# Matrix memory on one Trainium2 core: the key weights multiplied into the query weights on the chip

## The chip, the cores and the metric

One core of a Trainium2 chip (trn2) runs the whole program in one launch. The metric is the device time of one launch in microseconds; each measurement is the median of several runs. Five engines work side by side: TensorE (PE; its weight loads are listed as PEld), VectorE (DVE), ScalarE (ACT), GpSimd (POOL) and SyncE (SP), whose queue issues most DMAs.

## The reference

A trunk of two layers over 1024 tokens with 1024 features, in float32. The first layer has two mixers behind one input projection: a matrix memory (mLSTM, four heads of 256) and a pooling over trailing windows of 2, 4, 8 and 16 tokens (four groups of 256). The second layer is latent attention; the change does not touch it. What matters of the first layer:

```python
xc = silu(causal_conv(xm, conv_w, conv_b))          # per head h: (S, 256)
q = xc_h @ w_q[h]
k = xc_h @ w_k[h] * 256 ** -0.5
v = xm_h @ w_v[h]
# per chunk of tokens, with decays from the gates:
s = (q @ k.T) * exp(dmat - m_t)
num = s @ v + w_inter * (q @ C);   den = rowsum(s) + w_inter * (q @ n)
C_new = wc * C + (k * ws).T @ v;   n_new = wc * n + sum(k * ws)
h = num / max(|den|, exp(-m_t))
h = rms_norm(h * sigmoid(om)) ;    ya = (h + skip * xc) * silu(zm)
```

## The kernel before

*Numbers in two parts.* Every operand of a large matmul is held as a high part `hi` (float32r) and the remainder `lo`. `mm3` (L172) issues three matmuls for a product: hi*hi, hi*lo and lo*hi. Data in SBUF are split by `split` (POOL writes `hi`, DVE the remainder), data in PSUM by `split_psum` and `split_scaled` (ACT writes `hi`, DVE the remainder).

*Weights.* `wload` (L182) takes a staging tile, sends a DMA on SP's queue and splits the block on POOL and DVE. In this layer there are two staging tiles and three tiles each for `hi` and `lo`, used in turn. `head_w` (L681) loads the 256 x 256 matrix of a head.

*Projections.* `feat_pieces` (L320) gives 128 columns of the input projection, in two pieces of 24 matmuls (512 tokens each). It is a generator: each `run(gen, n)` issues n pieces more, so that pieces can stand between other steps. `fill` holds the four pieces of the pooled input (`xp_pieces`), `zp_pieces` two per feature tile of the pooling gate, `xm_pieces` the memory's input, `zm_pieces` its gate; `om_tile` makes the output gate, 24 matmuls of 256 columns for each of eight token tiles.

*Heads and chunks.* The loop at L684 runs over the heads 3, 2, 1, 0. A head has two chunks of 512 tokens. `conv` makes `xc` (features on partitions), `Chunk.v` the values, `Chunk.kq` keys and queries (24 + 24 matmuls of 512 columns over both chunks, `k_ps` and `q_ps`), `decay` the exponentials, `scores` the lower triangle of the scores (`s_ps`), `update` the state after the first chunk: it transposes the keys (`kT_ps`), weights them and multiplies them with the values (`st`). `outputs` multiplies scores with values (`n_ps`), in the second chunk also queries with the state (`i_ps`), and normalises; `turn` transposes the result (`hT_ps`) and adds the skip. `windows` computes the trailing means on POOL and DVE, `pool_out` multiplies them with the group's weights (`pool_ps`).

*PSUM.* Two pools: `pmm` with five tiles for products and `ptr` with three for transposes.

*Order.* The program's text gives priorities. A planner with a simulated timeline (`schedule_with_timeline_sim`) sets the order on each engine from them, so instructions that are ready in its simulation can pass others; on the chip each engine then runs its list in order. Buffers are given out in the order of the text, and a tile's next user waits for its last reader.

The calls of a head whose order is changed, before:

```python
        c0.v(x_0, wv)
        ch_0 = c0.split_x(xc0)
        x_1 = c0.split_x(xm[:, :, 3 + HALF:3 + S])
        wq, wk = head_w("a_w_q", h), head_w("a_w_k", h)
        c0.kq(ch_0, wk, wq)
        skip_scale(h, xc0)
        c0.decay(); run(fill, 1); c0.scores()
        upd = c0.update(); run(upd, 1); run(fill, 1); run(upd)
        c0.outputs(sig); run(fill, 1)
        ...                                  # chunk 1: wv, wq, wk loaded again
        run(zp_pieces(g, 0, zs)); c1.scores()
        pool_out(g, 0, wg, mixes, zs); c1.outputs(sig)
```

The functions with the profile's line numbers:

Of the kernel before, what the change touches and what calls it, by code (L numbers as in the profile page):

```python
# [56 lines left out]
def _parts(value, bits, n):  # L57
    """value as a sum of n numbers of at most `bits` significant bits each."""
    from fractions import Fraction
    out = []  # L60
    rest = value
    top = 0
    while Fraction(2) ** (top + 1) <= rest:
        top += 1
    lsb = top - bits + 1
    for _ in range(n):
        unit = Fraction(2) ** lsb
        q = int(rest / unit)
        out.append(float(q * unit))
        rest -= q * unit  # L70
        lsb -= bits
    return out
# [16 lines left out]
def _hybrid(ctx, tc, nc, ins, consts, out, dbg):  # L89
# [20 lines left out]
    # ---------------------------------------------------------------- constants  # L110
# [5 lines left out]
    rows = cp.tile([P, P], F32, name="rows")  # L116
# [22 lines left out]
    def load_columns():  # L139
# [23 lines left out]
    def split_scaled(hi, lo, src, scale):  # L163
        """src * scale = hi + lo; src in PSUM, scale a number or a column."""
# [7 lines left out]
    def mm3(acc, terms, start=True, stop=True):  # L172
        """acc (+)= sum of lhs.T @ rhs over terms ((lhs_hi, lhs_lo), (rhs_hi, rhs_lo))."""
# [8 lines left out]
    def wload(shape, src, hi_eng="pool", own=None, into=None):  # L182
        """A block of weights, or of other operands, loaded and split."""
# [25 lines left out]
    def rstd_of(dst, ssq, n):  # L209
        """dst = (ssq / n + eps) ** -0.5 for small tiles."""  # L210
# [7 lines left out]
    # ================================================================ layer A  # L218
# [29 lines left out]
    def om_tile(h, sig, ws, j):  # L248
        """sigmoid(om) of a head for 128 tokens; with the last head's columns the gates too."""
# [12 lines left out]
    # ---- x normalised, transposed and split, and the first head's output gate on its heels  # L262
    with pool("xload") as tp:
# [43 lines left out]
        for j in range(NT):  # L307
# [5 lines left out]
            if j == 5:  # L313
                load_columns()
# [5 lines left out]
    def feat_pieces(c0, use, w=None):  # L320
        """128 columns of the projection, features on partitions: use(half, psum) per half."""
# [16 lines left out]
    def xm_pieces(h, xm, ws=(None, None)):  # L338
        V.memset(xm[:, :, 0:3], 0.0)
        for f in range(2):  # L340
            def use(half, ps):
                A.copy(xm[:, f, 3 + half * HALF:3 + (half + 1) * HALF], ps[:])
            yield from feat_pieces(A_XM + h * HD + f * P, use, ws[f])

    def new_xm():
        xm = hp.tile([P, 2, 3 + S], F32, name="xm", tag="xm", bufs=1)
        return xm

    def conv(h, c, xm):
        """SiLU of the causal convolution of a chunk."""  # L350
        t0 = c * HALF
        xc = hp.tile([P, 2, HALF], F32, name="xc", tag="xc", bufs=2)
        for f in range(2):
            ft = 2 * h + f
            acc = xc[:, f, :]
            A.activation(acc, xm[:, f, t0 + 3:t0 + 3 + HALF], AF.Identity,
                         bias=gcol("conv_b", ft), scale=gcol("conv_w", 3 * 8 + ft))
            for tap in range(3):
                V.scalar_tensor_tensor(acc, xm[:, f, t0 + tap:t0 + tap + HALF], gcol("conv_w", tap * 8 + ft),
# [4 lines left out]
    def xp_pieces(g, x0s):  # L364
        for f in range(2):
            x0 = hp.tile([P, PAD + S], F32, name="px", tag="px", bufs=2)
# [7 lines left out]
    def windows(g, x0s, half):  # L374
        """Trailing means less the value itself, split, for half of the tokens."""
# [44 lines left out]
    def gate_math():  # L420
# [4 lines left out]
        # Scratch in the room of tiles that come later.  # L425
# [13 lines left out]
        # log_sigmoid(f) = min(f, 0) - log1p(exp(-|f|))  # L439
# [10 lines left out]
        # Sums of log f within a tile of 128 tokens, and over whole tiles.  # L450
# [19 lines left out]
        # The running maximum within a tile, one (tile, head) per partition; then over tiles.  # L470
# [26 lines left out]
        # Exponents of the decay that depend on the query, as rows.  # L497
# [16 lines left out]
        # Weights of the first chunk's tokens in the state, and of the state later.  # L514
# [11 lines left out]
    # The next weights land behind x; their split stays behind x's work too.  # L526
# [8 lines left out]
    class Chunk:  # L535
        """One head's mLSTM over 512 tokens, step by step."""
# [6 lines left out]
        def split_x(self, src):  # L543
            xh = hb.tile([P, 2, HALF], F32R, name="xh", tag="xh", bufs=2)
            xl = hb.tile([P, 2, HALF], F32R, name="xl", tag="xl", bufs=2)
            for f in range(2):
                split(xh[:, f, :], xl[:, f, :], src[:, f, :])
            return xh, xl

        def v(self, xhl, wv):  # L550
            """Values, tokens on partitions, with a column of ones for the denominators."""
# [4 lines left out]
            V.tensor_copy(vl[:, :, HD:HD + 2], vzero[:].unsqueeze(1).broadcast_to([P, 4, 2]))  # L556
            for jj in range(2):
# [7 lines left out]
            self.vh, self.vl = vh, vl  # L565

        def kq(self, chl, wk, wq):
            ch, cl = chl
            self.qh = qh = hb.tile([P, 2, HALF], F32R, name="qh", tag="qh", bufs=1)
            self.ql = ql = hb.tile([P, 2, HALF], F32R, name="ql", tag="ql", bufs=1)  # L570
            self.kh = kh = hb.tile([P, 2, HALF], F32R, name="kh", tag="kh", bufs=1)
            self.kl = kl = hb.tile([P, 2, HALF], F32R, name="kl", tag="kl", bufs=1)
            if self.c == 0:
                self.kf = kf = hb.tile([P, 2, HALF], F32, name="kf", tag="hs", bufs=1)
            for f in range(2):
                fs = slice(f * P, (f + 1) * P)
                ps = pmm.tile([P, 512], F32, name="k_ps", tag="mm")
                mm3(ps[:], [((wk[0][:, k, fs], wk[1][:, k, fs]), (ch[:, k, :], cl[:, k, :])) for k in range(2)])
                if self.c == 0:
                    A.activation(kf[:, f, :], ps[:], AF.Copy, scale=HD ** -0.5)  # L580
                    split(kh[:, f, :], kl[:, f, :], kf[:, f, :])
                else:
                    split_scaled(kh[:, f, :], kl[:, f, :], ps[:], HD ** -0.5)
                ps = pmm.tile([P, 512], F32, name="q_ps", tag="mm")
                mm3(ps[:], [((wq[0][:, k, fs], wq[1][:, k, fs]), (ch[:, k, :], cl[:, k, :])) for k in range(2)])
                split_psum(qh[:, f, :], ql[:, f, :], ps[:])

        def decay(self):
            """exp of the decays' exponents, zero above the diagonal; keys on partitions."""
# [20 lines left out]
        def update(self):  # L610
            """The state after the first chunk."""
            h, kf, vh, vl = self.h, self.kf, self.vh, self.vl
            sth = hb.tile([P, 2, HD + 2], F32R, name="sth", tag="sth", bufs=1)
            stl = hb.tile([P, 2, HD + 2], F32R, name="stl", tag="stl", bufs=1)
            kwh = hb.tile([P, 4, HD], F32R, name="kwh", tag="kh", bufs=1)
            kwl = hb.tile([P, 4, HD], F32R, name="kwl", tag="kl", bufs=1)
            for i in range(4):
                pt = ptr.tile([P, 512], F32, name="kT_ps", tag="tr")
                for f in range(2):
                    T.transpose(pt[:, f * P:(f + 1) * P], kf[:, f, i * P:(i + 1) * P], ident[:])  # L620
# [12 lines left out]
        def outputs(self, sig):  # L633
            """Gated head outputs, tokens on partitions, and their norms."""
# [3 lines left out]
            for j in range(4):  # L638
# [8 lines left out]
                if self.state is not None:  # L647
                    sth, stl = self.state
                    pi = pmm.tile([P, 512], F32, name="i_ps", tag="mm")
# [12 lines left out]
                A.activation(sq[:], hs[:, j, :], AF.Square, accum_out=ssq[:, j:j + 1])  # L662
            rs = hb.tile([P, 4], F32, name="h_rs", tag="h_rs", bufs=2)
# [4 lines left out]
        def turn(self, xc):  # L668
            """Normalised outputs to features on partitions, plus the skip."""
# [13 lines left out]

    for h in reversed(range(M_HEADS)):  # L684
# [7 lines left out]
        x_0 = c0.split_x(xm[:, :, 3:3 + HALF])  # L692
        xc1 = conv(h, 1, xm)
        if h == M_HEADS - 1:
# [8 lines left out]
        c0.v(x_0, wv)  # L703
        ch_0 = c0.split_x(xc0)
        x_1 = c0.split_x(xm[:, :, 3 + HALF:3 + S])
        wq, wk = head_w("a_w_q", h), head_w("a_w_k", h)
        c0.kq(ch_0, wk, wq)
        skip_scale(h, xc0)
        c0.decay()
        run(fill, 1)  # L710
        c0.scores()
        upd = c0.update()
        run(upd, 1)
        run(fill, 1)
# [12 lines left out]
        skip_scale(h, xc1)  # L727
# [15 lines left out]
    # ---- output projection of layer A, half of the tokens at a time  # L743
# [35 lines left out]
    def norm_stats(tp, srcs):  # L779
        """Four tiles of 128 tokens, normalised in place."""  # L780
# [9 lines left out]
    def norm_turn(srcs, gname, hi_of, lo_of):  # L790
        """... and transposed, with a gain per feature, to hi_of(k), lo_of(k) : [128, 512]."""
# [55 lines left out]
    # ================================================================ layer C  # L847
# [37 lines left out]
    def rope(rp, src, cg, sg, n, eng):  # L885
        """Rotates src [128, n, 64] with tables that carry the gains; a float32 tile."""
# [9 lines left out]
    def rope_tables(rp, cgk, sgk):  # L896
# [16 lines left out]
        # ang - k1 * (4096 * 2 pi) - k2 * 2 pi, with products and differences that are exact  # L913
        # down to the last bits, for any 32-bit position.
# [432 lines left out]
```

## Time and profile before

| | |
|---|---|
| median of 3 runs | 1405.29 us (1404.62 to 1405.62) |
| span of the profiled execution | 1403.8 us |
| its own time outside the span | not listed; the median is 1.5 us above the span |
| instructions | 20224 |
| TensorE busy | 1374.9 us, 98% |
| DVE, ACT, POOL busy | 755.2, 475.0, 412.0 us |
| the four heads of the memory | up to about 638 us of the span |

The profile shows one execution. A row of a group gives line, engine, operation, output and inputs, shape, count, then busy time and mean duration in ns, then the idle time ahead of it and what ended that. The durations of matmuls overlap, so the sum of durations is more than the time they take. A row of the order of time gives start and duration in us, and in brackets an idle time of the engine ahead of it with what released it.

### The profile page before, as it was taken

Reading aid. Unit: us, or ns where it says so; the run is one execution under the profiler, and the core shown is the slowest. Engines: PE = TensorE matmul, PEld = TensorE weight load, DVE = VectorE, ACT = ScalarE, POOL = GpSimd, SP = SyncE. Lnnn points to the kernel's source line nnn. Section 1 sums busy time; section 2 is a strip of 40 time slices with the busy share of each in tenths; the row PEclk is TensorE's granted clock in tenths of the full one; section 3 lists DMA queues with packets and bytes.
Section 4 is the critical chain, followed back from the end, with each engine's and each line's share of the span. In section 5 each row is a group of like instructions: output and inputs, shape, how many; then the busy total and the mean of one; then the engine's idle time right before and its main releaser. Section 6 shows DMA issues by size and latency. Waiting matters only on the chain.

```text
span 1403.8 us, 20224 instructions
## 1 busy us (share of the span) xinstructions
PE 1374.9 (98%) x7740; PEld 1205.8 (86%) x7740; DVE 755.2 (54%) x1616; ACT 475.0 (34%) x1146; POOL 412.0 (29%) x546
## 2 busy tenths in 40 slices
PE   7999999999999999999999999999989999999998
PEld 6888789888998889888888889988889999988887
DVE  6686544663365544653655333640167777878631
ACT  5433223331432223320001112421376667675200
POOL 3155213441144212321533111420153324151310
PEclk9999999999999999999999999999999999999999
DMA  5122311133022311127834232231311211122541
GB/s 198 39 81 64 101 53 48 55 94 97 16 80 60 102 53 53 51 74 253 301 106 150 90 88 78 73 103 53 104 34 54 67 54 54 57 80 69 217 157 53
DMA packets 101406, 126.88 MB, mean 90 GB/s; under 512 B 6231, under 2 KB 72510, under 8 KB 101310
## 3 DMA queue, kind: packets, MB, share of 16 engines
q1 hardware_dynamic: 98574, 115.63, 25.9%
q10 hardware_dynamic: 2736, 9.96, 2.0%
q8 instruction: 61, 1.00, 0.3%
q14 instruction: 35, 0.29, 0.1%
HBM read 100.34 MB, written 25.24 MB: 89 GB/s over the span
## 4 chain that ended last, share of the span: by engine, by line
PE 88%; DVE 4%; POOL 2%; issue 2%; DMA 2%; ACT 2%; SPq 0%; DVEq 0%; ACTq 0%; POOLq 0%
PE fp_ps L178 8%; PE fp_ps L177 8%; PE fp_ps L176 8%; PE s_ps L1155 5%; PE o_ps L176 4%; PE o_ps L178 4%; PE o_ps L177 4%; PE z_ps L178 2%; PE z_ps L177 2%; PE z_ps L176 2%; PE f_ps L178 2%; PE f_ps L176 2%; PE f_ps L177 2%; PE om_ps L177 2%; PE om_ps L178 2%; PE om_ps L176 2%
## 5 line engine op out<-in xcount | busy, mean ns | idle before, releaser
L156 POOL TENSOR_SCALAR w_hi<-w_st 128x1024 fp32r<-128x1024 f32 (+4 forms) x131 | 134.2, 1025 | 555.8 <-PE fp_ps L177 136.7
L161 DVE TENSOR_TENSOR w_lo<-w_st,w_hi 128x1024 fp32r<-128x1024 f32 (+4 forms) x131 | 156.2, 1194 | 221.7 <-POOL w_hi L156 221.7
L178 PE MATMUL fp_ps<-xnh,w_lo 128*128 128x512 f32 x512 | 202.6, 398 | 0.8 <-DVE w_lo L161 0.7
L177 PE MATMUL fp_ps<-xnl,w_hi 128*128 128x512 f32 x512 | 202.6, 396 | 0.0
L176 PE MATMUL fp_ps<-xnh,w_hi 128*128 128x512 f32 x512 | 202.1, 395 | 0.1
L178 PEld LDWEIGHTS fp_ps<-xnh,w_lo 128*128 128x128 f32 x512 | 96.1, 188 | 23.3 <-DVE w_lo L161 2.0
L176 PEld LDWEIGHTS fp_ps<-xnh,w_hi 128*128 128x128 f32 x512 | 97.2, 190 | 21.9 <-DVE zp L407 0.3
L177 PEld LDWEIGHTS fp_ps<-xnl,w_hi 128*128 128x128 f32 x512 | 96.2, 188 | 21.9
L178 PE MATMUL o_ps<-w_hi,yl 128*128 128x512 f32 x256 | 100.6, 393 | 0.0
L177 PE MATMUL o_ps<-w_lo,yh 128*128 128x512 f32 x256 | 100.4, 392 | 0.0
L176 PE MATMUL o_ps<-w_hi,yh 128*128 128x512 f32 x256 | 99.3, 395 | 0.0
L176 PE MATMUL om_ps<-w_hi,xnh 128*128 128x256 f32 (+1 forms) x256 | 73.1, 287 | 1.2 <-POOL w_hi L156 1.1
L177 PE MATMUL om_ps<-w_lo,xnh 128*128 128x256 f32 (+1 forms) x256 | 73.1, 287 | 0.1
L178 PE MATMUL om_ps<-w_hi,xnl 128*128 128x256 f32 (+1 forms) x256 | 73.0, 286 | 0.0
L1162 ACT ACTIVATE sp<-sp,mx,rq 128x128 f32<-128x128 f32 (+3 forms) x64 | 55.5, 867 | 22.3 <-DVE mx L1161 21.8
L178 PEld LDWEIGHTS o_ps<-w_hi,yl 128*128 128x128 f32 x256 | 48.1, 188 | 11.2
L177 PEld LDWEIGHTS o_ps<-w_lo,yh 128*128 128x128 f32 x256 | 48.1, 188 | 10.8
L176 PEld LDWEIGHTS o_ps<-w_hi,yh 128*128 128x128 f32 x256 | 48.1, 188 | 10.7
L170 DVE TENSOR_TENSOR ptl<-pT_ps,pth 128x512 fp32r<-128x512 f32 (+2 forms) x96 | 51.2, 548 | 6.1 <-ACT pth L169 6.0
L176 PEld LDWEIGHTS om_ps<-w_hi,xnh 128*128 128x128 f32 x256 | 49.1, 192 | 2.0 <-POOL w_hi L156 1.5
L176 PE MATMUL z_ps<-x1h,w_hi 128*128 128x512 f32 x128 | 50.7, 396 | 0.0
L178 PE MATMUL z_ps<-x1h,w_lo 128*128 128x512 f32 x128 | 50.7, 397 | 0.0
(364 smaller groups left out, 3594.3 us busy)
## 6 DMA issues: line engine op xcount, KB each, us to landing
w_st<-in_a_w_in_dram SPq DMA_DIRECT2D x38, 512.0 KB
w_st<-in_a_w_out_dram SPq DMA_DIRECT2D x32, 512.0 KB
w_st<-y_d SPq DMA_DIRECT2D x16, 512.0 KB
rb<-rr_d SPq DMA_DIRECT2D x8, 640.0 KB
x_t<-in_x_dram SPq DMA_DIRECT2D x8, 512.0 KB
y_d<-zp SPq DMA_DIRECT2D x16, 256.0 KB
y_d<-xc SPq DMA_DIRECT2D x16, 256.0 KB
x1t<-in_x_dram SPq DMA_DIRECT2D x8, 512.0 KB
```

Of the source, the lines that this page charges most:

```text
L156: i = G.tensor_scalar(hi, src, 1.0, 1.0, ALU.mult, ALU.mult)
L161: return i, V.tensor_tensor(lo, src, hi.bitcast(F32), ALU.subtract)
L170: V.tensor_tensor(lo, src, hi.bitcast(F32), ALU.subtract)
L176: T.matmul(acc, lh, rh, start=start and i == 0, stop=False)
L177: T.matmul(acc, lh, rl, start=False, stop=False)
L178: T.matmul(acc, ll, rh, start=False, stop=stop and i == n - 1)
L1155: T.matmul(ps[:, 0:w], l[:, js], r_[:, cs], start=i == 0, stop=i == 4)
L1162: A.activation(sp[:, 0:n], sp[:, 0:n], AF.Exp, bias=mx[:, 2:3], scale=rq[:, jt:jt + 1], accum_out=mx[:, 3:4])
```

## The change

The scores are q k^T = xc (Wq Wk^T) xc^T. The new kernel computes A = Wq Wk^T / 16 once per head on the chip (`qk_weights`): it transposes both weight matrices on TensorE, splits them out of PSUM and multiplies them. The queries are made with A (`Chunk.q`), and the split `xc` (`split_c`, in the tiles `kh`, `kl`) stands where the keys stood: in the scores, and through its transposes in the state. The key product and the second loading of the query and key weights are gone.

The steps of a head are also ordered anew: values in two halves around the product A, pieces of `fill` between scores, state and outputs, `outputs` in two halves with pieces of the pooling gate between them. `i_ps` comes from the pool `ptr`. The second chunk's input is split earlier, `skip_scale` of chunk 0 runs later, the weighted keys take the tiles `xh`, `xl`. The memory's input lies in two tiles that share three slots with the pooled input, and the tile of constant rows lies in the pool that loads x. Comments are dropped throughout.

```diff
+        def split_c(self, xc):
+            self.xc = xc
+            self.kh, self.kl = self.split_x([xc[:, f, :] for f in range(2)], ("kh", "kl"), 1)
...
-        def kq(self, chl, wk, wq):
+        def q(self, ws):
+            ch, cl = self.kh, self.kl
...
-                ps = pmm.tile([P, 512], F32, name="k_ps", tag="mm")
-                mm3(ps[:], [((wk[0][:, k, fs], wk[1][:, k, fs]), (ch[:, k, :], cl[:, k, :])) for k in range(2)])
-                if self.c == 0:
-                    A.activation(kf[:, f, :], ps[:], AF.Copy, scale=HD ** -0.5)
-                    split(kh[:, f, :], kl[:, f, :], kf[:, f, :])
-                else:
-                    split_scaled(kh[:, f, :], kl[:, f, :], ps[:], HD ** -0.5)
...
-                mm3(ps[:], [((wq[0][:, k, fs], wq[1][:, k, fs]), (ch[:, k, :], cl[:, k, :])) for k in range(2)])
+                mm3(ps[:], [((ws[0][:, k, fs], ws[1][:, k, fs]), (ch[:, k, :], cl[:, k, :])) for k in range(2)])
...
-            kwh = hb.tile([P, 4, HD], F32R, name="kwh", tag="kh", bufs=1)
+            kwh = hb.tile([P, 4, HD], F32R, name="kwh", tag="xh", bufs=2)
...
-                    T.transpose(pt[:, f * P:(f + 1) * P], kf[:, f, i * P:(i + 1) * P], ident[:])
+                    T.transpose(pt[:, f * P:(f + 1) * P], xc[:, f, i * P:(i + 1) * P], ident[:])
...
-                    pi = pmm.tile([P, 512], F32, name="i_ps", tag="mm")
+                    pi = ptr.tile([P, 512], F32, name="i_ps", tag="tr")
...
+    def qk_weights(h, res):
+        wt = []
+        for name in ("a_w_q", "a_w_k"):
+            wp, WN, nst, nsp = wpool["now"]
+            st = wp.tile([P, WN], F32, name="w_st", tag="w_st", bufs=nst)
+            sv = st[:, 0:2 * HD].rearrange("p (k n) -> p k n", n=HD)
+            SY.dma_start(sv, ins[name][0, h].rearrange("(k p) n -> p k n", p=P))
+            hi = wp.tile([P, WN], F32R, name="w_hi", tag="w_hi", bufs=nsp)
+            lo = wp.tile([P, WN], F32R, name="w_lo", tag="w_lo", bufs=nsp)
+            ps = ptr.tile([P, 512], F32, name="wT_ps", tag="tr")
+            for d in range(2):
+                for k in range(2):
+                    T.transpose(ps[:, d * HD + k * P:d * HD + (k + 1) * P], sv[:, k, d * P:(d + 1) * P], ident[:])
+            split_psum(hi[:, 0:2 * HD], lo[:, 0:2 * HD], ps[:])
+            wt.append([t[:, 0:2 * HD].rearrange("p (k n) -> p k n", n=HD) for t in (hi, lo)])
+        yield
+        (qh, ql), (kh, kl) = wt
+        ah = hb.tile([P, 2, HD], F32R, name="ah", tag="ah", bufs=1)
+        al = hb.tile([P, 2, HD], F32R, name="al", tag="al", bufs=1)
+        ps = pmm.tile([P, 512], F32, name="a_ps", tag="mm")
+        for f in range(2):
+            fs = slice(f * P, (f + 1) * P)
+            mm3(ps[:, f * HD:(f + 1) * HD], [((qh[:, d, fs], ql[:, d, fs]), (kh[:, d, :], kl[:, d, :])) for d in range(2)])
+        flat = "p k n -> p (k n)"
+        split_scaled(ah[:].rearrange(flat), al[:].rearrange(flat), ps[:], HD ** -0.5)
+        res += [ah, al]
...
+        x_1 = c0.split_x([t[:, PAD + HALF:PAD + S] for t in xm])
...
-        c0.v(x_0, wv)
-        ch_0 = c0.split_x(xc0)
-        x_1 = c0.split_x(xm[:, :, 3 + HALF:3 + S])
-        wq, wk = head_w("a_w_q", h), head_w("a_w_k", h)
-        c0.kq(ch_0, wk, wq)
-        skip_scale(h, xc0)
+        wa = []
+        qk = qk_weights(h, wa)
+        run(qk, 1)
+        v0 = c0.v(x_0, wv)
+        run(v0, 1)
+        run(qk)
+        run(v0)
+        c0.split_c(xc0)
+        c0.q(wa)
         c0.decay()
         run(fill, 1)
         c0.scores()
+        run(fill, 1)
         upd = c0.update()
         run(upd, 1)
+        skip_scale(h, xc0)
+        out0 = c0.outputs(sig)
+        run(out0, 1)
         run(fill, 1)
         run(upd)
-        c0.outputs(sig)
-        run(fill, 1)
+        run(out0)
+        run(fill)
         wv = head_w("a_w_v", h)
-        wq, wk = head_w("a_w_q", h), head_w("a_w_k", h)
         c1 = Chunk(h, 1, c0.after)
         c1.decay()
-        c1.v(x_1, wv)
-        ch_1 = c1.split_x(xc1)
+        c1.split_c(xc1)
+        run(c1.v(x_1, wv))
+        c1.q(wa)
+        skip_scale(h, xc1)
         c0.turn(xc0)
-        run(fill)
-        c1.kq(ch_1, wk, wq)
-        skip_scale(h, xc1)
...
-        run(zp_pieces(g, 0, zs))
+        zp = zp_pieces(g, 0, zs)
+        run(zp, 1)
         c1.scores()
+        run(zp)
+        out1 = c1.outputs(sig)
+        run(out1, 1)
+        zs1 = []
+        zp = zp_pieces(g, 1, zs1)
+        run(zp, 1)
+        run(out1)
         pool_out(g, 0, wg, mixes, zs)
-        c1.outputs(sig)
-        zs = []
-        run(zp_pieces(g, 1, zs))
-        pool_out(g, 1, wg, mixes, zs)
+        run(zp)
+        pool_out(g, 1, wg, mixes, zs1)
```

More of the change, by code (lines that the diff above doesn't have):

```diff
@@ L114, in _hybrid @@
     V.tensor_copy(identr[:], ident[:])
-    rows = cp.tile([P, P], F32, name="rows")
     col = {}
@@ L137, in _hybrid, with load_columns @@
     cols = cp.tile([P, P], F32, name="cols")
-    def load_columns():
+    def load_columns(tp):
+        rows = tp.tile([P, P], F32, name="rows", bufs=1)
         G.memset(rows[:], 0.0)
@@ L313, in _hybrid @@
             if j == 5:
-                load_columns()
+                load_columns(tp)
         om_tile(M_HEADS - 1, sig3, ws, NT - 1)
@@ L338, in xm_pieces @@
     def xm_pieces(h, xm, ws=(None, None)):
-        V.memset(xm[:, :, 0:3], 0.0)
         for f in range(2):
+            x0 = xm[f]
+            V.memset(x0[:, PAD - 3:PAD], 0.0)
             def use(half, ps):
-                A.copy(xm[:, f, 3 + half * HALF:3 + (half + 1) * HALF], ps[:])
+                A.copy(x0[:, PAD + half * HALF:PAD + (half + 1) * HALF], ps[:])
             yield from feat_pieces(A_XM + h * HD + f * P, use, ws[f])
     def new_xm():
-        xm = hp.tile([P, 2, 3 + S], F32, name="xm", tag="xm", bufs=1)
-        return xm
+        return [hp.tile([P, PAD + S], F32, name="xm", tag="px", bufs=3) for _ in range(2)]
     def conv(h, c, xm):
@@ L355, in conv @@
             acc = xc[:, f, :]
-            A.activation(acc, xm[:, f, t0 + 3:t0 + 3 + HALF], AF.Identity,
+            A.activation(acc, xm[f][:, t0 + PAD:t0 + PAD + HALF], AF.Identity,
                          bias=gcol("conv_b", ft), scale=gcol("conv_w", 3 * 8 + ft))
             for tap in range(3):
-                V.scalar_tensor_tensor(acc, xm[:, f, t0 + tap:t0 + tap + HALF], gcol("conv_w", tap * 8 + ft),
+                V.scalar_tensor_tensor(acc, xm[f][:, t0 + PAD - 3 + tap:t0 + PAD - 3 + tap + HALF], gcol("conv_w", tap * 8 + ft),
                                        acc, ALU.mult, ALU.add)
@@ L365, in xp_pieces @@
         for f in range(2):
-            x0 = hp.tile([P, PAD + S], F32, name="px", tag="px", bufs=2)
+            x0 = hp.tile([P, PAD + S], F32, name="px", tag="px", bufs=3)
             G.memset(x0[:, 0:PAD], 0.0)
@@ L541, in __init__, with split_x @@
             SY.dma_start(self.rb[:], rr_d[h:h + 1, c, :].to_broadcast([P, TRI[4]]))
-        def split_x(self, src):
-            xh = hb.tile([P, 2, HALF], F32R, name="xh", tag="xh", bufs=2)
-            xl = hb.tile([P, 2, HALF], F32R, name="xl", tag="xl", bufs=2)
+        def split_x(self, srcs, tags=("xh", "xl"), bufs=2):
+            xh = hb.tile([P, 2, HALF], F32R, name="xh", tag=tags[0], bufs=bufs)
+            xl = hb.tile([P, 2, HALF], F32R, name="xl", tag=tags[1], bufs=bufs)
             for f in range(2):
-                split(xh[:, f, :], xl[:, f, :], src[:, f, :])
+                split(xh[:, f, :], xl[:, f, :], srcs[f])
             return xh, xl
+        def split_c(self, xc):
+            self.xc = xc
+            self.kh, self.kl = self.split_x([xc[:, f, :] for f in range(2)], ("kh", "kl"), 1)
         def v(self, xhl, wv):
@@ L556, in v @@
             V.tensor_copy(vl[:, :, HD:HD + 2], vzero[:].unsqueeze(1).broadcast_to([P, 4, 2]))
+            self.vh, self.vl = vh, vl
             for jj in range(2):
@@ L564, in v @@
                 split_psum(vh[:, 2 * jj:2 * jj + 2, 0:HD], vl[:, 2 * jj:2 * jj + 2, 0:HD], pv)
-            self.vh, self.vl = vh, vl
-        def kq(self, chl, wk, wq):
-            ch, cl = chl
+                yield
+        def q(self, ws):
+            ch, cl = self.kh, self.kl
             self.qh = qh = hb.tile([P, 2, HALF], F32R, name="qh", tag="qh", bufs=1)
             self.ql = ql = hb.tile([P, 2, HALF], F32R, name="ql", tag="ql", bufs=1)
-            self.kh = kh = hb.tile([P, 2, HALF], F32R, name="kh", tag="kh", bufs=1)
-            self.kl = kl = hb.tile([P, 2, HALF], F32R, name="kl", tag="kl", bufs=1)
-            if self.c == 0:
-                self.kf = kf = hb.tile([P, 2, HALF], F32, name="kf", tag="hs", bufs=1)
             for f in range(2):
                 fs = slice(f * P, (f + 1) * P)
-                ps = pmm.tile([P, 512], F32, name="k_ps", tag="mm")
-                mm3(ps[:], [((wk[0][:, k, fs], wk[1][:, k, fs]), (ch[:, k, :], cl[:, k, :])) for k in range(2)])
-                if self.c == 0:
-                    A.activation(kf[:, f, :], ps[:], AF.Copy, scale=HD ** -0.5)
-                    split(kh[:, f, :], kl[:, f, :], kf[:, f, :])
-                else:
-                    split_scaled(kh[:, f, :], kl[:, f, :], ps[:], HD ** -0.5)
                 ps = pmm.tile([P, 512], F32, name="q_ps", tag="mm")
-                mm3(ps[:], [((wq[0][:, k, fs], wq[1][:, k, fs]), (ch[:, k, :], cl[:, k, :])) for k in range(2)])
+                mm3(ps[:], [((ws[0][:, k, fs], ws[1][:, k, fs]), (ch[:, k, :], cl[:, k, :])) for k in range(2)])
                 split_psum(qh[:, f, :], ql[:, f, :], ps[:])
@@ L610, in update @@
         def update(self):
-            h, kf, vh, vl = self.h, self.kf, self.vh, self.vl
+            h, xc, vh, vl = self.h, self.xc, self.vh, self.vl
             sth = hb.tile([P, 2, HD + 2], F32R, name="sth", tag="sth", bufs=1)
             stl = hb.tile([P, 2, HD + 2], F32R, name="stl", tag="stl", bufs=1)
-            kwh = hb.tile([P, 4, HD], F32R, name="kwh", tag="kh", bufs=1)
-            kwl = hb.tile([P, 4, HD], F32R, name="kwl", tag="kl", bufs=1)
+            kwh = hb.tile([P, 4, HD], F32R, name="kwh", tag="xh", bufs=2)
+            kwl = hb.tile([P, 4, HD], F32R, name="kwl", tag="xl", bufs=2)
             for i in range(4):
@@ L662, in outputs @@
                 A.activation(sq[:], hs[:, j, :], AF.Square, accum_out=ssq[:, j:j + 1])
+                if j == 1:
+                    yield
             rs = hb.tile([P, 4], F32, name="h_rs", tag="h_rs", bufs=2)
@@ L682, in head_w @@
         return wload([P, 2, HD], ins[name][0, h].rearrange("(k p) n -> p k n", p=P))
+    def qk_weights(h, res):
[13 more added lines that the diff above has]
+            wt.append([t[:, 0:2 * HD].rearrange("p (k n) -> p k n", n=HD) for t in (hi, lo)])
+        yield
+        (qh, ql), (kh, kl) = wt
[8 more added lines that the diff above has]
+        res += [ah, al]
     for h in reversed(range(M_HEADS)):
@@ L691, in _hybrid @@
         c0 = Chunk(h, 0, None)
-        x_0 = c0.split_x(xm[:, :, 3:3 + HALF])
+        x_0 = c0.split_x([t[:, PAD:PAD + HALF] for t in xm])
         xc1 = conv(h, 1, xm)
+        x_1 = c0.split_x([t[:, PAD + HALF:PAD + S] for t in xm])
         if h == M_HEADS - 1:
```

## The prediction

> **What bounds the kernel now.** I read the page's busy table first, then a table of stages with the TensorE alone, then TensorE's list of waits, and last the order of time inside one head.
>
> ```profile
> PE 1374.9 (98%) x7740; PEld 1205.8 (86%) x7740; DVE 755.2 (54%) x1616; ACT 475.0 (34%) x1146; POOL 412.0 (29%) x546
> 43.00:81.00 38.00, 37.34 (x176) 1.00 0.17 49
> 81.00:166.00 85.00, 81.21 (x446) 1.00 0.24 74
> 166.00:323.50 157.50, 157.50 (x879) 1.00 0.23 68
> 323.50:480.90 157.40, 157.40 (x880) 1.00 0.23 67
> 480.90:638.40 157.50, 157.50 (x879) 1.00 0.21 63
> ```
>
> Columns of the stage rows: stretch, its length, TensorE busy (matmuls), granted clock, DMA share, GB/s. Heads 2, 1 and 0 take 157.5 us each and TensorE never stands idle in them, at full clock. There only fewer or shorter matmuls can save time. The first head (number 3, up to 166 us) is different: 3.8 us of its last 85 are idle. A busy share alone would mislead, because durations of matmuls overlap; the pace is read from starts.
>
> ```profile
> 233.31 0.28 PE L176 MATMUL v_ps<-w_hi,xh 128*128 128x256 f32 x1
> ...
> 236.13 0.39 PE L176 MATMUL k_ps<-xh,w_hi 128*128 128x512 f32 x1
> ...
> 241.68 0.40 PE L176 MATMUL fp_ps<-xnh,w_hi 128*128 128x512 f32 x1
> ...
> 479.83 0.39 PE L178 MATMUL pool_ps<-mh,w_lo 128*128 128x512 f32 x1
> 480.06 1.03 PE L674 MATMUL hT_ps<-ident,hs 128*128 128x128 f32 x8
> 480.86 0.47 PE L176 MATMUL fp_ps<-xnh,w_hi 128*128 128x512 f32 x1
> 481.17 0.39 PE L177 MATMUL fp_ps<-xnl,w_hi 128*128 128x512 f32 x1
> ```
>
> Each row: start, duration, line, out<-in, shape, count. From 233.31 to 236.13 stand the 24 value matmuls with 256 columns: 2.82 / 24 = 0.118 us each, though one lasts 0.28. From 236.13 to 241.68 stand 12 key and 12 query matmuls with 512 columns: 5.55 / 24 = 0.231 us each. Eight transposes take from 480.06 to 480.86, 0.80 us, and the matmul behind them is 0.31 instead of 0.23 from its successor: 0.88 us for a block of eight.
>
> **The change, part by part, for each of four heads.**
>
> *Keys.* Twelve key matmuls per chunk go, 24 a head: 24 x 0.231 = 5.55 us less on TensorE. With them go their evictions, none of which TensorE waits for in heads 2 to 0.
>
> *Folded weights.* Added are eight transposes of the raw query and key weights (bounded by the hT block: 0.88 us) and 12 matmuls of 256 columns for the product (value rows: 12 x 0.118 = 1.41 us). Balance on TensorE: -5.55 + 0.88 + 1.41 = **-3.26 us a head, -13.0 us for four.** Chunk 1 uses the same product, so nothing is paid twice.
>
> The Trainium skill, in "TensorE: Matmul & The Clock Gate", Part 4, puts a PE transpose in a kernel at about 275 ns and says the full clock does not engage for it. The hT rows, 0.10 us from start to start at clock 1.00, do not bear that out as a pace; by the page the 32 transposes would be an estimated 8.8 us instead of 3.5 and the saving 7.8 us.
>
> *Loads and splits.*
>
> ```profile
> L169 ACT CAST vh<-v_ps 128x512 fp32r<-128x512 f32 x16 | 9.3, 587 | 12.1 <-PE v_ps L178 12.1
> L170 DVE TENSOR_TENSOR vl<-v_ps,vh 128x512 fp32r<-128x512 f32 x16 | 11.0, 684 | 12.0 <-ACT vh L169 12.0
> L580 ACT ACTIVATE kf<-k_ps x8: 597/599/602, 87.7 to 555.3; 128x512 f32<-128x512 f32 x8
> L166 DVE SCALAR_TENSOR_TENSOR kl<-k_ps,kh x8: 673/677/693, 118.3 to 598.7; 128x512 fp32r<-128x512 f32 x8
> L156 POOL TENSOR_SCALAR w_hi<-w_st 128x512 fp32r<-128x512 f32 x36 | 23.5, 653 | 209.5 <-PE om_ps L178 60.7 <-PE kv_ps L178 47.6 <-issue 39.5
> L161 DVE TENSOR_TENSOR w_lo<-w_st,w_hi 128x512 fp32r<-128x512 f32 x36 | 27.9, 776 | 75.6 <-POOL w_hi L156 75.6
> L156 POOL TENSOR_SCALAR kh<-kf 128x512 fp32r<-128x512 f32 x8 | 8.5, 1068 | 3.3 <-ACT kf L580 3.3
> L161 DVE TENSOR_TENSOR kl<-kf,kh 128x512 fp32r<-128x512 f32 x8 | 9.9, 1245 | 0.0
> 202.23 0.38 SPq L202 DMA_DIRECT2D w_st<-in_a_w_q_dram  x1
> 212.48 0.37 SPq L202 DMA_DIRECT2D w_st<-in_a_w_k_dram  x1
> ```
>
> POOL loses four weight splits and two key splits a head, 4 x 0.65 + 2 x 1.07 = 4.8 us. DVE loses 4 x 0.78 + 2 x 1.25 + 2 x 0.68 = 7.0 and gains three subtractions, 3 x 0.68 = 2.0. ACT loses four key evictions and gains three (two casts at 0.59, the scaled one at 0.60). SP's queue issues two 256 KB loads fewer a head. All of it is beside TensorE, so I cost it at nothing; if the cover were gone, the sign would still be a gain. The first chunk's query and key weights are issued at 202 and 212 us and the head needs them at 233: the transposes, which now stand in TensorE's own queue ahead of the values, do not wait for DMA.
>
> *The new chain.* Query of chunk 0 now needs: transposes, cast of the key weights (0.59), subtraction (0.68), product (1.41 on TensorE), its scaled eviction (0.60), subtraction (0.68), then the first query matmuls. The two open legs are 0.59 + 0.68 = 1.27 and 0.60 + 0.68 = 1.28 us. The code sets half of the values behind each: 12 x 0.118 = 1.41 us. Each leg is covered with 0.13 us to spare, so 0 by these rows; uncovered it is 2.55 a head. I take 0, nearer to the covering rows.
>
> *Weight slots behind it.* The weight pool has three split slots, used in turn.
>
> ```profile
> 232.14 0.62 POOL L156 TENSOR_SCALAR w_hi<-w_st 128x512 fp32r<-128x512 f32 x1 [20.23 <-PE om_ps L178]
> 237.56 1.35 POOL L156 TENSOR_SCALAR w_hi<-w_st 128x1024 fp32r<-128x1024 f32 x1
> 239.36 1.21 DVE L161 TENSOR_TENSOR w_lo<-w_st,w_hi 128x1024 fp32r<-128x1024 f32 x1
> L156 POOL TENSOR_SCALAR w_hi<-w_st 128x1024 fp32r<-128x1024 f32 x83 | 96.1, 1158 | 279.8 <-PE fp_ps L177 103.8 <-PE o_ps L178 65.5 <-PE z_ps L177 47.3
> L161 DVE TENSOR_TENSOR w_lo<-w_st,w_hi 128x1024 fp32r<-128x1024 f32 x83 | 112.6, 1360 | 127.3 <-POOL w_hi L156 127.3
> ```
>
> POOL sat 20 us until the output gate's matmuls released a slot. The next projection piece takes the slot of the value weights, released when the values end. Before, 5.55 us of key and query matmuls followed; now only the queries, 12 x 0.231 = 2.78. Its split needs 1.16 + 1.36 us, and one query subtraction (0.68) may stand ahead on DVE: 3.20. Open: 0.42 us a head, +1.7 for four. Between 0 (eight state transposes, ready by then, step in) and 0.42 I take 0.42, since the queue is in order.
>
> *Waits added and moved.* Chunk 1's split of the convolved input now waits for chunk 0's scores to release the key tiles; behind it on POOL are the window sums, and a piece of 24 matmuls (24 x 0.231 = 5.5 us) lies between. The scaling by skip moves behind the state's transposes on ACT; its reader, the turned output, is a chunk later. The weighted keys take the slots of the values' input, released by the values, early. Gated numerators move to the other PSUM pool, of three tiles, which only transposes share there. The second half of the input is split earlier, under the output gate, where POOL's 20 us of idling (row above) hide it; without that cover it would cost two POOL splits, about 1.3 us. Projection pieces stand between scores, state and outputs instead of behind them: the same matmuls, so 0 where nothing idles. xm in the three pooled slots: a slot is reused a head later, when its window sums are long done; 0. The constant rows move to the pool of x: 0.
>
> *The first head.* There idle time can be won.
>
> ```profile
> 80.98:166.03 85.05, 81.26 (x447) 1.00 0.24 74
> 233.31:323.53 90.22, 90.22 (x495) 1.00 0.26 74
> PE pool_ps L176 <- POOL px L367: 1.8, 1, 1.8
> PE hT_ps L674 <- DVE hs L666: 1.1, 2, 0.8
> PE n_ps L176 <- POOL sh L156: 0.5, 1, 0.5
> ```
>
> The second row is the same work of head 2, with 48 more projection matmuls (48 x 0.231 = 11.1): the first head loses 85.05 - 79.1 = 5.9 us. The last rows are TensorE's waits in the first stretch. The pooling matmul's 1.8 and the numerators' 0.5 should go, since a piece of the gate now stands ahead of both: -2.3. The transposes of hs lose 2.8 us of key matmuls ahead of them, so their wait is between 1.1 less and 2.8 more; I take +0.8. Sum -1.5; ends -3.4 and +0.5, and -5.9 if the whole loss went.
>
> **Sum.** -13.0 + 1.7 - 1.5 = -12.8. The profiled execution spans 1403.8 us, 1.5 under the median of the runs, 1405.29; the difference is taken from both alike: 1392.5.
>
> **Rivals.**
>
> 1. *The chain stays open.* If the values run ahead of the transposes or the casts queue, 2.55 us a head come back: (-3.26 + 2.55) x 4 - 1.5 = -4.3, 1401; one leg open, 1396. For it: margins of 0.13 us. Against it: DVE and ACT are at 54% and 34%.
>
> 2. *Slower, by the clock.*
>
> ```profile
> 1030.00:1049.40 19.40, 16.47 (x95) 0.82 0.16 44
> 1038.75 0.45 PE L1181 MATMUL pT_ps<-ident,sp 128*128 128x128 f32 x1 [1.96 <-DVE sp L1164]
> ```
>
> In attention TensorE idled 2.9 us of this stretch, and the granted clock fell to 0.82: about 7 us at half speed, some 3.5 us lost. If the open chain (2.55) and the slot wait (0.42) stand together in each head and set this off, a head pays 2.97 + 3.5 - 3.26 = +3.2; with nothing won in the first head, 1418. It decides from 3.26 us lost a head. Against it: the 3.8 us idle in the first head, spread out, left the clock at 1.00, and it would have to happen in all heads.
> The Trainium skill, same page, Part 1, states such a gate: about 3.4 us of idling halves the clock. The stretch above agrees in kind.
>
> 3. *All goes well.* The first head loses nothing and no wait is new: -13.0 - 5.9 = 1386.4.
>
> 4. *Each transpose costs its whole duration.*
>
> ```profile
> L674 PE MATMUL hT_ps<-ident,hs 128*128 128x128 f32 x64 | 8.7, 274 | 1.1 <-DVE hs L666 1.1
> ```
>
> At 0.274 instead of 0.11 us, 32 of them cost 5.3 us more: 1398. This is the page's rule named above; the 0.80 us for eight speak against it.
>
> 5. *No change.* New waits of about 3 us a head, without the clock, eat the gain: 1402.5 to 1408.
>
> **How the numbers follow.** No change means within 0.2% (2.8 us), about what a measurement here can tell. The sum of the rows: 0.62; rival 1: 0.15; rival 3: 0.09; rival 4: 0.02; these are faster, 0.88. Rival 5: 0.06, rival 2: 0.06. From 1386 (rival 3) to 1399 (one leg open and rival 4 within) leaves out rivals 2 and 5 and half of rival 1, some 0.2.
>
> **What would show it.** Right: heads 2 to 0 at about 154.6 us each; no k_ps; 32 transposes of the weights at 0.1 us from start to start; the product at 0.118; few TensorE waits at the first query matmul and the first projection piece. Wrong: TensorE waiting on ACT or DVE at the product or the query, a granted clock below 1.00 before 640 us, or the first head longer than 82 us between its values and its end.

## The result, and the profile after

| | before | after |
|---|---|---|
| median | 1404.95 us (1403.76 to 1405.62, 4 runs) | 1389.57 us (1388.54 to 1391.10, 4 runs) |
| span of the profiled execution | 1403.8 us | 1389.4 us |

The ratio is 0.9895, interval [0.9881, 0.9909]: 15.4 us faster by the medians, 14.4 by the profiles. The forecast was 1392.5, range 1386 to 1399. The number is near; the experiments show that one step behind it was wrong, and that the change could as well have brought nothing.

The page's busy line after, and the table of the heads with TensorE alone (stretch, length, busy and matmuls, granted clock, DMA share, GB/s; from the first head's values to the last head's end, a head ending at the first matmul behind its last transposes of `hs`):

```profile
PE 1361.1 (98%) x7724; PEld 1195.2 (86%) x7724; DVE 742.3 (53%) x1600; ACT 470.9 (34%) x1142; POOL 397.5 (29%) x522
81.09:159.26 78.17, 77.02 (x442) 1.00 0.27 80
159.26:313.97 154.71, 154.46 (x875) 1.00 0.22 65
313.97:469.01 155.04, 154.79 (x875) 1.00 0.22 65
469.01:624.33 155.32, 155.07 (x876) 1.00 0.21 61
```

The first row was 85.05 and is 78.17: 6.9 us less. Heads 2 to 0 took 157.5, 157.3 and 157.4 us from one such boundary to the next and take 154.7, 155.0 and 155.3: 2.8, 2.3 and 2.1 less. What follows the heads is 0.5 us shorter, and the values begin 0.1 later: 14.4 in all.

The new chain in head 2, in order of time (start, duration, line, out<-in, count, and in brackets TensorE's wait), with two rows of DVE's list:

```profile
226.59 1.03 PE L696 MATMUL wT_ps<-ident,w_st 128*128 128x128 f32 x8
...
232.15 0.60 PE L617 MATMUL kT_ps<-ident,xc 128*128 128x128 f32 x4
233.00 0.50 PE L176 MATMUL q_ps<-xh,ah 128*128 128x512 f32 x1 [0.25 <-ACT ah L165]
...
234.03 0.40 PE L176 MATMUL fp_ps<-xnh,w_hi 128*128 128x512 f32 x1
```

```profile
232.81 1.22 DVE L161 TENSOR_TENSOR w_lo<-w_st,w_hi 128x1024 fp32r<-128x1024 f32 x1 [0.37 <-POOL w_hi L156]
...
234.35 0.68 DVE L166 SCALAR_TENSOR_TENSOR al<-a_ps,ah 128x512 fp32r<-128x512 f32 x1
```

The eight transposes begin at 226.59, the values behind them 0.79 us later. The transposes of the state were put into what was left of the gaps, and 0.25 us of wait remains at the queries. The remainder of the product (`al`) stands on DVE behind a weight split of 1.22 us and is ready only at 235.0; TensorE's list has four query matmuls that need only `ah`, then a projection piece at 234.03, and finishes the queries later.

### The profile page after: what moved, and what is told of

It reads as the page before. It is cut to its first block, busy times and chain, and to the rows that moved or that the text cites. A ratio compares the mean times of both kernels' runs of the same rounds, so it can differ in the third digit from the quotient of the medians.

```text
span 1389.4 us, 20100 instructions
## 1 busy us (share of the span) xinstructions
PE 1361.1 (98%) x7724; PEld 1195.2 (86%) x7724; DVE 742.3 (53%) x1600; ACT 470.9 (34%) x1142; POOL 397.5 (29%) x522
## 4 chain that ended last, share of the span: by engine, by line
PE 91%; DVE 3%; ACT 2%; POOL 1%; issue 1%; DMA 1%; SPq 0%; DVEq 0%; ACTq 0%; POOLq 0%
PE fp_ps L176 8%; PE fp_ps L178 8%; PE fp_ps L177 8%; PE s_ps L1194 5%; PE o_ps L177 4%; PE o_ps L176 4%; PE o_ps L178 4%; PE z_ps L178 2%; PE z_ps L177 2%; PE z_ps L176 2%; PE f_ps L176 2%; PE f_ps L178 2%; PE f_ps L177 2%; PE om_ps L176 2%; PE om_ps L178 2%; PE om_ps L177 2%
## 5 line engine op out<-in xcount | busy, mean ns | idle before, releaser
L156 POOL TENSOR_SCALAR w_hi<-w_st 128x1024 fp32r<-128x1024 f32 (+4 forms) x115 | 125.7, 1094 | 549.2 <-PE fp_ps L177 110.8
L161 DVE TENSOR_TENSOR w_lo<-w_st,w_hi 128x1024 fp32r<-128x1024 f32 (+4 forms) x115 | 142.6, 1242 | 168.7 <-POOL w_hi L156 168.4
```

The lines of the kernel that those rows point to most:

```text
L156: i = G.tensor_scalar(hi, src, 1.0, 1.0, ALU.mult, ALU.mult)
L161: return i, V.tensor_tensor(lo, src, hi.bitcast(F32), ALU.subtract)
```

## The experiments

### The folding alone

The changed kernel with the steps of a head, and the PSUM pool of `i_ps`, as before the change; the fold with the halved values around it stays. So do the smaller parts of the change: the tiles that share slots, the early split of the second input and `skip_scale` behind the state's transposes.

```diff
-        run(fill, 1)
         upd = c0.update()
         run(upd, 1)
         skip_scale(h, xc0)
-        out0 = c0.outputs(sig)
-        run(out0, 1)
         run(fill, 1)
         run(upd)
-        run(out0)
-        run(fill)
+        run(c0.outputs(sig))
+        run(fill, 1)
...
-                    pi = ptr.tile([P, 512], F32, name="i_ps", tag="tr")
+                    pi = pmm.tile([P, 512], F32, name="i_ps", tag="mm")
```

> The changed kernel with the steps of a head in the old order (pieces of the pooled input, pooling gate, pooling products and outputs as before, the state's numerators in the old PSUM pool); only the folded weights with the values in two halves around them are kept. Theory A, the gain is the balance of TensorE's matmuls: 13.0 us less than before, less some 1.6 us of waits in the new chain, so 1393 to 1394 us, with the first head losing its old 6 us. Rival B, the gain comes from the new order of the steps and the folding mostly pays for itself: 1400 us or more.

Measured: 1406.54 us beside 1405.95 before, ratio 1.0013 [1.0003, 1.0023]. The whole gain was gone. In all eleven executions the mean granted clock was 0.993 to 0.996. Its heads 2 to 0, then the transfer of the decay's rows as SP's queue issues it in head 1, and ACT, DVE and TensorE behind it:

```profile
160.13:319.06 158.93, 156.31 (x873) 0.99 0.22 64
319.06:482.19 163.13, 158.37 (x874) 0.98 0.22 62
482.19:641.87 159.68, 156.71 (x874) 0.99 0.20 59
```

```profile
411.92 0.34 SPq L542 DMA_DIRECT2D rb<-rr_d  x1
```

```profile
416.06 1.28 ACT L590 ACT_TABLE_LOAD   x1 [3.62 <-DMA rb<-rr_d]
417.35 0.72 ACT L590 ACTIVATE rb<-rb,bs 128x512 f32<-128x512 f32 x1
417.98 0.35 ACT L169 CAST sth<-st 128x258 fp32r<-128x258 f32 x1
```

```profile
418.37 0.43 DVE L170 TENSOR_TENSOR stl<-st,sth 128x258 fp32r<-128x258 f32 x1 [2.31 <-ACT sth L169]
```

```profile
416.56 0.28 PE L178 MATMUL n_ps<-vh,sl 128*128 128x258 f32 x1
418.85 0.39 PE L176 MATMUL n_ps<-vh,sh 128*128 128x258 f32 x1 [2.01 <-DVE stl L170]
```

Read from the top: the rows for the next chunk's decay are issued when the scores, which lie in the same tile, have been read. ACT stands 3.62 us at the head of its list, waiting for them to land, then loads a table and does an exponential; the state's copy, whose input was ready, comes behind; DVE's remainder behind that; and TensorE, which wants the PSUM tile, has waited 2.01 us. In the second chunk the next head's rows do the same to the numerators' copies (TensorE waits 2.50 us there). Then the clock, in stretches of some 3.4 us around that wait:

```profile
416.80:419.70 2.90, 0.89 (x7) 0.98 0.14 44
419.70:423.10 3.40, 3.40 (x14) 0.52 0.00 0
423.10:426.50 3.40, 3.40 (x16) 1.00 0.00 0
```

After the idle time the clock is at half for one stretch of 3.4 us. This happens four times in heads 2 to 0, behind waits of 2.37, 2.01, 2.50 and 2.73 us. The waits sum to 9.6 us, and four such stretches cost an estimated 6.8 (3.4 x 0.5 each): 16.4 together, more than the 13.0 that the folding was to save over four heads. Measured, heads 2 to 0 take 481.7 us (641.87 - 160.13) instead of the changed kernel's 465.1 (624.33 - 159.26): 16.6 more.

### The new order alone

Keys, queries and weights as before the change, in the new order.

```diff
-        wa = []
-        qk = qk_weights(h, wa)
...
-        c0.q(wa)
+        run(c0.v(x_0, wv))
+        ch_0 = c0.split_x([xc0[:, f, :] for f in range(2)])
+        wq, wk = head_w("a_w_q", h), head_w("a_w_k", h)
+        c0.kq(ch_0, wk, wq)
```

> The new order of the steps with keys, queries and their weights as before the change. Theory A: heads 2 to 0, where TensorE never stood idle, stay at 157.5 us each, and only the first head gains some 3.6 us: 1401 to 1402 us. Rival B: 1395 us or less.

Measured: 1409.47 us, ratio 1.0029 [1.0018, 1.0040] (its profile spans 1406.1). Not the expected 1401. TensorE's waits up to the end of the heads add up to 6.4 us, and the longest entry is this:

```profile
PE k_ps L176 <- POOL xh L156: 2.8, 4, 0.9
```

The early split of the second input takes the free slot of `xh`, so the split of the convolved input, which the keys need, waits for the values. That is an effect of this mixture: in the changed kernel that split has tiles of its own. So it was run again with the second input split at its old place.

> The new order without folding as in the earlier run, but the second half of the input is split at its old place, behind the split of the convolved input, so that the latter finds a free slot. Theory A: heads 2 to 0 go back to 157.5 us each and the first head keeps its gain: 1401 to 1403 us. If the new order itself costs something without folding: 1406 us or more.

Measured: 1403.13 us, ratio 0.9992 [0.9982, 1.0001]. Heads, the boundaries here at the transposes of `hs`, about 0.8 us earlier than in the table above:

```profile
80.90:162.28 81.38, 79.39 (x440) 1.00 0.26 77
162.28:319.82 157.54, 157.54 (x878) 1.00 0.23 67
319.82:478.23 158.41, 157.95 (x878) 1.00 0.23 67
478.23:636.61 158.38, 157.97 (x877) 1.00 0.21 63
```

Between the same two steps as in the table above (81.22 to 163.07) the first head takes 81.85 us instead of 85.05, a gain of 3.2; the others gain nothing or lose 1. Alone, the order with its input split at the old place is worth at most 0.2%, and the folding less than nothing; together they are worth 15 us.

### What held the folding back

First the transfer was taken out of the fold-only kernel.

```diff
-            self.rb = hb.tile([P, TRI[4]], F32, name="rb", tag="rb", bufs=1)
-            SY.dma_start(self.rb[:], rr_d[h:h + 1, c, :].to_broadcast([P, TRI[4]]))
+            if "t" not in rb_once:
+                rb_once["t"] = hb.tile([P, TRI[4]], F32, name="rb", tag="rb", bufs=1)
+                SY.dma_start(rb_once["t"][:], rr_d[h:h + 1, c, :].to_broadcast([P, TRI[4]]))
+            self.rb = rb_once["t"]
```

> The fold-only kernel with the decay's rows (rb) loaded once in the whole program instead of once per chunk; later chunks apply the exponential in place, with the row's term multiplied by 0, so this kernel leaves the later chunks' true decays out. The number of exponentials and all other work stay. Theory D: the fold-only kernel lost its 13 us because ScalarE stood at the head of its list waiting for the rb transfer (4.07 us from issue to landing), the state's or numerators' copies behind it came late, TensorE idled 2 to 2.5 us and its clock fell to half for 3.41 us; without the transfer heads 2 to 0 fall from 159 to 163 us to about 155 us and the time to 1392 to 1396 us. Rival E: the old order starves TensorE in another way (PSUM tiles, VectorE): 1402 us or more.

Measured: 1393.57 us, ratio 0.9924 [0.9909, 0.9939].

```profile
159.58:314.32 154.74, 154.49 (x874) 1.00 0.20 57
314.32:469.34 155.02, 154.77 (x873) 1.00 0.20 57
469.34:624.47 155.13, 154.88 (x873) 1.00 0.20 57
```

The heads are those of the changed kernel, in the old order. Then the transfer was left in place and only ACT's list was mended: its copies of state and numerators and its exponentials are kept in the order of the text.

```diff
-                A.activation(rb[:, tr], rb[:, tr], AF.Exp, bias=bs[:, 4 * c + i, h:h + 1])
+                tc.keep_in_program_order(A.activation(rb[:, tr], rb[:, tr], AF.Exp, bias=bs[:, 4 * c + i, h:h + 1]))
...
+                tc.keep_in_program_order(A.copy(sth[:, f, :], acc[:, 0:HD + 2]))
...
+                    tc.keep_in_program_order(A.activation(num[:], pi[:, 0:HD + 2], AF.Copy, scale=wint[:, j, h:h + 1]))
```

> The fold-only kernel, all work and data as in it, with one change of order: ScalarE's copies of the state, its copies of the numerators and the exponentials of the decay are kept in the order of the text, so that the exponentials that wait for the rb transfer stand behind the copies and not ahead of them. Theory D (head of ScalarE's list blocked by the transfer): the waits of 2.0 to 2.7 us on TensorE and the half clock behind them go, heads 2 to 0 at about 155 us, 1392 to 1396 us, as with the transfer left out. If the transfer itself were the limit whatever the order: 1402 us or more.

Measured: 1392.98 us, ratio 0.9915 [0.9900, 0.9930]. Head 1 of its table of stages, and ACT's list in that head:

```profile
314.27:469.65 155.38, 155.02 (x874) 1.00 0.23 65
```

```profile
409.92 0.73 ACT L627 CAST sth<-st 128x258 fp32r<-128x258 f32 x2 [1.93 <-PE st L178]
...
419.97 1.92 ACT L590 ACTIVATE rb<-rb,bs 128x512 f32<-128x512 f32 x4
```

The copies now stand 10 us ahead of the exponentials, and the head takes 155.4 instead of 163.1 us. TensorE's list in this head is the same as with the folding alone, except for the order of a few score matmuls. The mean granted clock was 0.998 to 1.000 in the four executions. So the old order as such did not hold the folding back; the place of the exponentials in ACT's list did. What the new order adds to this is some 3 us by the medians (1389.57), and the intervals of the two ratios overlap. As a control, the transfer was also taken out of the changed kernel.

> The changed kernel with the rows of the decay loaded once (the row's term multiplied by 0 in later chunks, so their true decays are left out). Control: if the new order covers the transfer, as theory D says, nothing changes, 1388 to 1391 us; if ScalarE's waits for it still reach TensorE, 1385 us or less.

Measured: 1391.36 us, ratio 0.9903 [0.9886, 0.9919]: no gain. It is not that ACT waits less for the rows in the changed kernel. Its waits for them in heads 2 to 0 (us in total, times, longest), before, with the folding alone, and changed:

```profile
ACT L593 <- DMA rb<-rr_d: 4.9, 5, 1.5
ACT L590 <- DMA rb<-rr_d: 13.3, 5, 3.6
ACT L590 <- DMA rb<-rr_d: 29.2, 5, 10.0
```

ACT waits longest in the fastest kernel. But there pieces of the projection stand between the scores and the state's matmuls, so that in head 1 the state's copy, behind a wait of 3.32 us for the rows, still has to wait for TensorE:

```profile
415.15 0.73 ACT L169 CAST sth<-st 128x258 fp32r<-128x258 f32 x2 [0.66 <-PE st L178]
```

### What the new pieces cost

*The keys put back, unread.*

```diff
+                ps = pmm.tile([P, 512], F32, name="k_ps", tag="mm")
+                mm3(ps[:], [((ws[0][:, k, fs], ws[1][:, k, fs]), (ch[:, k, :], cl[:, k, :])) for k in range(2)])
                 ps = pmm.tile([P, 512], F32, name="q_ps", tag="mm")
```

> The changed kernel with the 96 matmuls of the key product issued again ahead of the queries' and never read. Theory A (TensorE's list is the bound, each matmul of 512 columns costs its pace of 0.231 us): 22.2 us more than the changed kernel, 1411 to 1412 us. If part of the removed work was cover for waits that are open now: less, 18 us or under.

Measured: 1411.78 us, ratio 1.0053 [1.0038, 1.0068]: 22.2 us above the changed kernel, which is 96 x 0.231. In the new order the removed matmuls are on the path, all of them as far as runs that differ by some 2 us can tell.

*Five times the transposes.*

```diff
-            for d in range(2):
-                for k in range(2):
+            for d, k in [(d, k) for _ in range(5) for d in range(2) for k in range(2)]:
+                if True:
```

> Each block of the query and key weights is transposed five times into the same place: 128 transposes more in all. By the pace from start to start (0.10 us) 12.8 us more, 1402 us; by the duration of each (0.274 us) 35 us more, 1425 us; 1390 us if TensorE has room beside other waits.

Measured: 1407.04 us (1403.53 to 1410.23), ratio 1.0006 [0.9996, 1.0016]; its profile spans 1401.8. The profile gives 12.4 us for 128 transposes, 0.097 each; the medians give 17.5, 0.137 each. Heads 2 to 0 in the profile:

```profile
163.66:322.01 158.35, 158.10 (x905) 1.00 0.21 64
322.01:480.66 158.65, 158.40 (x906) 1.00 0.22 64
480.66:639.55 158.89, 158.64 (x906) 1.00 0.20 59
```

They take 475.9 instead of 465.1 us: 10.8 / 96 = 0.113 each. The duration of 0.273 as a price (35 us) is excluded by both. Why the medians give 5 us more than the profiles is in part a matter of which execution was profiled: here the fastest of ten, the only one with a mean granted clock of 1.000 (the others 0.996 to 0.999), and of the changed kernel the longest of four. The heads are the better measure.

*All values ahead of the chain.*

```diff
-        run(qk, 1)
-        v0 = c0.v(x_0, wv)
-        run(v0, 1)
-        run(qk)
-        run(v0)
+        run(c0.v(x_0, wv))
+        run(qk)
```

> The changed kernel with all values of the first chunk ahead of the transposes of the weights, so that no half of them stands behind a leg of the new chain. Theory A with the cover as predicted: 2.55 us a head come back, about 1400 us. Rival C, other work that is ready (the state's transposes, a projection piece) steps in: at most 2 us more in all, 1390 to 1392 us.

Measured: 1398.75 us, ratio 0.9954 [0.9941, 0.9968], 9.2 us above the changed kernel (8.3 by the ratios). TensorE's rows with a wait of over 0.2 us around the product in head 1, and that head in the table of stages:

```profile
390.02 0.38 PE L176 MATMUL a_ps<-w_hi 128*128 128x256 f32 x1 [0.56 <-ACT w_hi L169]
393.22 0.50 PE L176 MATMUL q_ps<-xh,ah 128*128 128x512 f32 x1 [0.25 <-ACT ah L165]
395.47 0.50 PE L178 MATMUL fp_ps<-xnh,w_lo 128*128 128x512 f32 x1 [0.53 <-DVE w_lo L161]
```

```profile
317.10:474.43 157.33, 155.83 (x873) 1.00 0.22 64
```

The heads are 156.8, 157.3 and 157.6 us, 2.1 to 2.3 more than with the halves around the product. The cover is real; the transposes of the state fill only a part of it.

### The product under the output gate

A candidate: for heads 2 to 0 the transposes stand before the third and the product before the fifth tile of the output gate, in the tiles of the queries.

```diff
             for j in range(NT):
+                if j == 2:
+                    qk = qk_weights(h, wa)
+                    run(qk, 1)
+                if j == 4:
+                    run(qk)
                 om_tile(h, sig, ws, j)
```

> A candidate: for heads 2 to 0 the weights are transposed and multiplied between the tiles of the output gate, in tiles that the queries use later, so that the whole new chain lies under 22.6 us of matmuls. Waits around the chain in the changed kernel's heads 2 to 0 add up to some 0.5 us a head: 1.5 us less, 1388 us. No change if those waits only move to the weight slots behind.

Measured: 1390.20 us, ratio 0.9904 [0.9887, 0.9920]: the same as the changed kernel.

```profile
158.73:313.49 154.76, 154.76 (x873) 1.00 0.22 65
313.49:467.81 154.32, 154.32 (x873) 1.00 0.22 65
467.81:622.22 154.41, 154.41 (x873) 1.00 0.21 61
```

TensorE no longer idles in these heads, and 1.6 us less over three heads (463.5 for 465.1) is all that is left there; the runs cannot tell it.

## Why the prediction was right, and where not

*The balance of matmuls, -3.26 us a head: right, under a condition.* Each price stands: 0.231 for a key matmul (22.2 us for 96 put back), 0.11 for a transpose, and heads at 154.3 to 154.8 us when nothing waits (the candidate). The rule of the Trainium skill that the prediction weighed ("TensorE: Matmul & The Clock Gate", Part 4: about 275 ns for a transpose, no full clock) gave an estimated 7.8 us for the saving; the trace does not agree: 0.113 us each for 96 more of them, at clock 1.00.

*The open legs of the chain, 0: nearly right.* 0.25 us a head is left at the queries, and without the halves of the values around the product 2.1 to 2.3 us a head come back, where 2.55 were worked out.

*The weight slots, +0.42 a head: the wait is elsewhere.* The first projection piece does not wait for its weights in any head. It stands ahead of half the queries in TensorE's list, and the remainder of the product is ready only behind its start. In size, heads 2 to 0 lost 0.5 to 1.2 us of the 3.26, so 0.42 was a little low; that it is near at all is luck.

*The first head, -1.5: too small.* Beside the 3.3 of the balance it gained 3.6. The new order alone gives 3.2 there, but the folding in the old order with ACT's list mended also has 2.8 beyond the balance (79.02 us from 80.93 to 159.95). So it is not shown that the moved pieces win this time; the tiles and slots that both kernels share may. The wait of the transposes of hs, for which 0.8 was added, is gone from the list. In all, 4.3 us were forecast for this head and 6.9 measured, and for the three behind it 8.5 and 7.2: the sum is nearer than its terms, which is luck.

*"The same matmuls, so 0 where nothing idles": wrong.* This was the sentence on the pieces of `fill` and the gate. With the folding and these pieces at their old places, heads 2 to 0 take 16.6 us more. TensorE idled nowhere in them before, but ACT already waited there for the decay's rows. Its list in head 1, before, first with the state's copy and then in the second chunk:

```profile
417.07 1.28 ACT L593 ACT_TABLE_LOAD   x1 [1.07 <-DMA rb<-rr_d]
...
420.60 0.62 ACT L169 CAST sth<-st 128x258 fp32r<-128x258 f32 x2
```

```profile
463.39 0.46 ACT L653 ACTIVATE num<-i_ps,wint 128x258 f32<-128x258 f32 x1
465.36 1.28 ACT L593 ACT_TABLE_LOAD   x1 [1.51 <-DMA rb<-rr_d]
```

And the second chunk with the folding alone:

```profile
458.58 0.48 ACT L650 ACTIVATE num<-i_ps,wint 128x258 f32<-128x258 f32 x1 [6.96 <-PE i_ps L178]
461.81 1.28 ACT L590 ACT_TABLE_LOAD   x1 [2.75 <-DMA rb<-rr_d]
```

Before, the copy of the second numerators (463.39) stands ahead of the exponentials; with the folding alone only the first (458.58) does, and the second comes at 465.32, too late for TensorE. In the first chunk of head 1 the exponentials, or the first of them, stand ahead of the state's copy in both kernels, but with the folding the last of the state's matmuls starts 2.5 us behind the issue of the rows, before the change 5.9. With the old order the folding brings nothing (ratio 1.0013); the moved pieces made it pay, and keeping ACT's list in order does nearly the same. It is tempting to say that the removed matmuls had been the cover of the transfer. That is not shown: between the scores and the state of head 1 stand the same 24 projection matmuls before and with the folding alone, and no key matmul. The prediction asked which waits the new chain brings to TensorE, and put the other engines down at nothing; it did not ask what stands behind the transfers in their lists.

*Rival 2 named the right danger at the wrong place.* Idle time with the clock at half behind it did occur, four times, in the fold-only kernel: through the decay's transfer and ACT's list, not through the product. The same page of the Trainium skill, Part 1, gives about 3.4 us of idling as the condition for half clock; here waits of 2.0 to 2.7 us were enough.

## What to carry to other kernels

Taking work off a packed engine also changes what the other engines' lists look like and when their inputs come. Before counting such work as gain, list what waits on the other engines without harm so far, transfers first, and what stands behind those waits in each in-order list. Where a planner with modelled times makes the lists, an instruction that waits for a DMA may be put ahead of urgent copies; keeping three kinds of instructions in order was worth 13.6 us here, about as much as the folding itself. Measure the parts of a combined change apart, and ask of a part that is worth nothing what holds it back: here each alone was worth nothing, and yet the folding was worth 12 us once ACT's list was mended.

## What the runs showed of the hardware

TensorE's clock fell to half for one stretch of about 3.4 us after idle times of 2.0 to 2.7 us (the table above: 0.52 in 419.70 to 423.10, 1.00 behind it); a wait of 1.78 us in the first head before the change was not followed by it. A wait of 1.95 to 1.96 us behind the heads stands in all twelve profiles. The clock is at half behind it in seven, the kernel before and the changed one among them, and not in five, the new order alone among them. With all values ahead of the chain a wait of 1.84 us behind the heads was followed by it as well; so the length by itself doesn't decide. The executions of one kernel differ in the clock too: of 25 executions of the kernel before, in one of the sessions, the three with a mean granted clock of 1.000 took 1402.6 to 1403.4 us, the two with 0.996 took 1407.5 and 1407.6. Forty transposes in a row, 4.4 us, kept the clock at 1.00. What makes heads 1 and 0 of the changed kernel 0.3 and 0.6 us longer than head 2 was not looked into; the candidate's heads do not show it.
